# The order search of a hybrid GLA/RWKV-7 layer starts from a table of start times in the source

## Chip, core and metric

The kernel runs on one core of one Trainium2 chip. The metric is the device time of one execution in microseconds (us), the median of several runs. PE is the matmul engine (TensorE), DVE the vector engine (VectorE), ACT the scalar engine (ScalarE), POOL is GpSimd, SP is the queue engine (SyncE) that issues all DMAs here.

## Reference

One layer of a trunk with two groups of heads, on x of 4096 x 1024 in float32 (excerpt; sizes filled in):

```python
h = _rmsnorm(x, norm_w)
u = h @ w_in                          # one combined projection
# GLA group: 4 heads, key 64, value 128, chunks of 64
log_a = log_sigmoid(glr @ gate_up + gate_bias) / 16
o = _gla_chunked(q, k, v, log_a)
gla_out = rmsnorm_per_head(o) * silu(gg)
# RWKV-7 group: 8 heads of 64
mixed = cols + (prev_token(cols) - cols) * mu
r, rk, rv, wl, al = split(mixed)
# S_t = S_(t-1) (diag(w_t) - kk_t^T (a_t * kk_t)) + v_t^T k_t ;  y_t = S_t r_t
y = _rwkv7_scan(r, decay, k, v, kk, a)
rwkv_out = (groupnorm(y) + bonus) * silu(rg)
x = x + concat(gla_out, rwkv_out) @ w_out
return _rmsnorm(x, final_norm_w)
```

## The kernel before

**Tiles and stages.** The 4096 tokens go through in 8 blocks of 512. In each block the normalised x (tile `x`, two float16 halves) is multiplied by 29 tiles of 128 columns of the input weights, split into float16 high and low parts (`wr` for the RWKV group, `wg` for GLA, `wo` for the output); each projection matmul is one of three products of such halves. Weights are split once in the first 200 us, written to DRAM (`wdr`) and read back in every block through a few buffers. The RWKV group works in units of two heads: four per block, 32 in all, each of 8 chunks of 64 tokens. For a unit DVE makes `DD` (r and the normalised key with their decays) and `bk` (k and a with theirs); 16 matmuls `bank<-DD,bk` give the products within the chunks; the inverse of the delta rule's triangle is built from `Nb` and `Ta`. Then the chunks follow one upon another: `ch<-sv,DD` on PE, `us` copied out by ACT, `ch<-us,Nb`, `uv` copied out by ACT, `ch<-uv,bk`, and the new state `sv` made by DVE. That is three handovers a chunk, between PE and ACT or DVE, and each takes some time in which PE needs other matmuls to run: projections of the next block (`bank<-x,wr`, `bank<-x,wg`), or the output projection (`bank<-x,wo`). A finished block gets its residual, and its final RMSNorm, of which the last operations are eight DVE multiplies `mgg<-mgg,pkt,xacc` and `mgr<-mgr,pkt,xacc`, ahead of the store.

**What sets the order.** No instruction is emitted when it is written. Generators for the streams of work (named x, w, c, e, i, g, a, o, p, and one d for each unit; c is the chunk chain, a the projections and preparation of RWKV, p of GLA, o the output) call recording engines: every call (L473; pairs of matmuls on the two halves of the array L532) makes a `Step` with engine, a duration, and the steps that it depends on. In `build(guide)` the next stream to go on is that whose next step has the earliest start in `guide`; this decides also which buffer each tile gets. The key of a step is its stream and its number in it. Then `forward` makes a list schedule of all steps with a rank: where the array can stay in one form of matmul it prefers that by `keep`, and DVE and ACT may wait `look` us for a step of better rank; `backward` gives the latest times, which are the ranks of the next `forward`. Five such passes (`PASSES`) are made for each pair (`keep`, `look`) in `LOOKS`. The loop at the end does this for each entry of `ROUNDS`, hands the starts found to the next round as its `guide`, keeps the schedule with the earliest end by the planner's own durations, and emits the steps by their start.

Of the kernel before, what the change touches and what calls it, by code (L numbers as in the profile page):

```python
# [3 lines left out]

# [13 lines left out]
AX = mybir.AxisListType  # L18
# [3 lines left out]
P = 128  # L22
DM = 1024
KT = 8
TB = 512
C = 64
# [13 lines left out]
DL = 0.6  # L40
# [3 lines left out]
XL = 0.05  # L44
EL = 0.0
PB = {"ch": 1, "y": 1}
NBK = 6
NC = TB // C
LOOKS = ((1.0, 0.15),)
PASSES = 5  # L50
PUT_OFF = 1.0
ROUNDS = (LOOKS,) * 11
GUP = 2.0 ** 19
DECAY = math.exp(-0.5)

# [25 lines left out]
CK_GM = 896  # L81
CK_SEL = 1408
NCK = 1536


@with_exitstack
def hymba_kernel(ctx, tc, xT, wt, wg, wo, wua, gup, pk, ck, out):
    nc = tc.nc
    nc.scalar.preload_act_table_set("exp_and_others")
    NT = out.shape[1]  # L90
# [1498 lines left out]
        return steps, forward, backward  # L1589

    with tc.manual_schedule(engines={getattr(mybir.EngineType, e) for e in ("PE", "DVE", "Activation", "Pool", "SP")}):
        guide, best = {}, None
        for looks in ROUNDS:
            steps, forward, backward = build(guide)
            first_order = forward([s.t0 for s in steps])
            mine = first_order
            for keep, look in looks:
                start, end = first_order
                for _ in range(PASSES):
                    start, end = forward(backward(end), keep, look)  # L1600
                    mine = min(mine, (start, end), key=lambda x: max(x[1]))
            if best is None or max(mine[1]) < max(best[2]):
                best = (steps,) + mine
            guide = {s.key: (mine[0][s.n], mine[1][s.n]) for s in steps}
        steps, start, end = best
        for s in sorted(steps, key=lambda s: (start[s.n], s.n)):
            s.f()
# [3 lines left out]
def _layout(d):  # L1611
# [22 lines left out]
    i = np.arange(P)  # L1634
    ck = np.zeros((P, NCK), np.float32)
    ck[:64, CK_BONES] = 1
# [34 lines left out]
```

## Time and profile before

| | |
|---|---|
| time, median of three runs | 2221.82 us (2220.91 to 2226.53) |
| profiled execution | 2219.66 us, of which the profile's span is 2217.9 us |
| PE busy | 2130.2 us, mean granted clock 0.984 |
| DVE busy | 1705.3 us |
| ACT busy | 1249.9 us |
| POOL busy | 877.8 us |
| largest group on PE | `bank<-x,wr`: 6528 matmuls, 799.4 us |

Times in the profile are in us from the span's start. A row of the time line has start, length, engine, line, operation, `out<-in` by the program's names, how many instructions the row joins, and in square brackets the idle time of the engine just before it with what ended it. "PE waits for" rows give the whole idle time, how often, and the longest. The granted clock is the share of full speed at which PE ran. Lines L473 and L532 are those of the two recording helpers, so groups are told apart by tiles and not by lines.

### The profile page before, as it was taken

Reading aid. Unit: us, or ns where it says so; the run is one execution under the profiler, and the core shown is the slowest. Engines: PE = TensorE matmul, PEld = TensorE weight load, DVE = VectorE, ACT = ScalarE, POOL = GpSimd, SP = SyncE. Lnnn points to the kernel's source line nnn. Section 1 sums busy time; section 2 is a strip of 40 time slices with the busy share of each in tenths; the row PEclk is TensorE's granted clock in tenths of the full one; section 3 lists DMA queues with packets and bytes.
Section 4 is the critical chain, followed back from the end, with each engine's and each line's share of the span. In section 5 each row is a group of like instructions: output and inputs, shape, how many; then the busy total and the mean of one; then the engine's idle time right before and its main releaser. Section 6 shows DMA issues by size and latency. Waiting matters only on the chain.

```text
span 2217.9 us, 75008 instructions
## 1 busy us (share of the span) xinstructions
PE 2130.2 (96%) x30680; PEld 1365.4 (62%) x30680; DVE 1705.3 (77%) x3802; ACT 1249.9 (56%) x3229; POOL 877.8 (40%) x2212
## 2 busy tenths in 40 slices
PE   6899999999999999999999999999999999999997
PEld 2556675666755657656675566655666565755664
DVE  8988969588785777768777787858878588684976
ACT  7676675464645456455654556545465464655452
POOL 3462434525253451426425254442533525254400
PEclk8999999999999999999999999999999999999999
DMA  6786655455344643455434554345534465344443
GB/s 202 241 260 179 189 166 165 140 181 165 90 133 141 179 127 101 122 150 179 131 110 120 177 155 129 112 134 163 164 98 124 131 187 159 91 130 126 120 131 96
DMA packets 275454, 326.90 MB, mean 147 GB/s; under 512 B 131572, under 2 KB 132772, under 8 KB 275108
## 3 DMA queue, kind: packets, MB, share of 16 engines
q1 hardware_dynamic: 275108, 322.10, 49.5%
q8 instruction: 240, 3.93, 0.7%
q14 instruction: 106, 0.87, 0.1%
HBM read 276.94 MB, written 45.05 MB: 145 GB/s over the span
## 4 chain that ended last, share of the span: by engine, by line
PE 64%; DVE 19%; DMA 8%; ACT 4%; issue 3%; POOL 2%; SPq 1%; DVEq 0%; ACTq 0%; POOLq 0%
PE bank L532 51%; PE bank L473 8%; PE ch L532 3%; DMA xr<-in_xT_dram 3%; DVE DD L473 2%; DVE nta L473 1%; DVE bk L473 1%; SPq L473 1%; PE y L473 1%; DVE mgr L473 1%; DVE mgg L473 1%; PE y L532 1%; DVE x L473 1%; DMA wdr<-wo 1%; DVE Nb L473 1%
## 5 line engine op out<-in xcount | busy, mean ns | idle before, releaser
L532 PE MATMUL bank<-x,wr 128*64 128x512 f16 x6528 | 799.4, 382 | 8.2 <-ACT x L473 2.7
L473 POOL TENSOR_TENSOR tm<-Tc,f 128x60 f32<-128x60 f32 (+24 forms) x961 | 349.7, 364 | 614.3 <-DMA f<-nd 531.6
L532 PEld LDWEIGHTS <-wr 128*64 128x64 f16 x6528 | 359.8, 111 | 266.6 <-issue 30.7
L473 POOL TENSOR_TENSOR Tc<-Tc,tm 128x60 f32<-128x60 f32 (+24 forms) x961 | 361.2, 376 | 74.1
L532 PE MATMUL bank<-x,wg 128*64 128x512 f16 x3072 | 372.2, 381 | 4.6 <-DVE ki L473 2.0
L532 PE MATMUL bank<-x,wo 128*64 128x512 f16 x2976 | 354.8, 381 | 0.1
L473 POOL TENSOR_TENSOR xacc<-xacc,xr 128x512 f32<-128x512 f32 x98 | 130.3, 1330 | 365.4 <-ACT xr L473 195.8
L532 PEld LDWEIGHTS <-wg 128*64 128x64 f16 x3072 | 174.0, 110 | 123.8 <-issue 7.3
L473 DVE SCALAR_TENSOR_TENSOR sv<-ch,PC,psd 64x64 f32<-64x64 f32 x434 | 122.4, 282 | 145.9 <-PE ch L532 131.8
L532 PEld LDWEIGHTS <-wo 128*64 128x64 f16 x2976 | 161.6, 110 | 116.9 <-issue 4.3
L532 PEld LDWEIGHTS <-x 128*64 128x64 f16 x6240 | 190.1, 110 | 20.9 <-issue 9.4
L532 PE MATMUL bank<-wg,x 128*64 128x128 f16 x6144 | 196.4, 219 | 4.4 <-issue 2.7
L473 ACT ACTIVATE psd<-sv,PC 128x128 f32<-128x128 f32 x248 | 99.1, 399 | 164.6 <-DVE sv L473 142.8
L473 ACT COPY uv<-ch 64x64 f32<-64x64 f32 x496 | 101.7, 205 | 82.1 <-PE ch L532 73.2
L473 ACT COPY us<-ch 64x64 f32<-64x64 f32 x496 | 101.5, 205 | 59.0 <-PE ch L532 50.5
L473 ACT ACTIVATE sa<-bank,mu_s 128x512 f32<-128x512 f32 x104 | 71.4, 687 | 64.7 <-PE bank L532 63.2
L473 DVE COPY_PREDICATED Nb<-mc,bank 64x512 f32<-64x512 uint8 x128 | 92.9, 728 | 6.2 <-PE bank L473 4.4
L473 DVE COPY_PREDICATED DD<-mc,bank 64x512 f32<-64x512 uint8 x128 | 93.5, 731 | 2.7
L532 PEld LDWEIGHTS ch<-sv,DD 128*64 128x64 f32 x992 | 66.1, 138 | 47.0 <-DVE sv L473 15.0
L532 PEld LDWEIGHTS ch<-us,Nb 128*64 128x64 f32 x992 | 66.3, 138 | 45.8 <-ACT us L473 15.4
L532 PEld LDWEIGHTS ch<-uv,bk 128*64 128x64 f32 x992 | 66.1, 138 | 41.5 <-ACT uv L473 12.8
L473 POOL MEMSET Tc<- 32x8 f32 (+1 forms) x160 | 23.5, 147 | 165.5 <-DMA td<-Tc 160.1
(348 smaller groups left out, 3616.9 us busy)
## 6 DMA issues: line engine op xcount, KB each, us to landing
wr<-wdr SPq DMA_DIRECT2D x256, 256.0 KB
wg<-wdr SPq DMA_DIRECT2D x184, 256.0 KB
xr<-in_xT_dram SPq DMA_DIRECT2D x176, 256.0 KB
wo<-wdr SPq DMA_DIRECT2D x128, 256.0 KB
f<-nd SPq DMA_DIRECT2D x128, 128.0 KB
x<-in_wt_dram SPq DMA_DIRECT2D x29, 512.0 KB
wdr<-wo SPq DMA_DIRECT2D x25, 512.0 KB
out_dram<-mgg SPq DMA_DIRECT2D x33, 256.0 KB
```

The lines of the kernel that those rows point to most:

```text
L473: put(t0, self.name, d, lag, cols, tiles, tab, outs, ins, lambda: f(*a, **kw))
L532: nc.tensor.matmul(x, lhsT=l, rhs=y, start=start, stop=stop)
```

## The change

The starts of the first guide come from a table in the source: 25,340 differences in tenths of a us, one for each step, packed; `COUNTS` names 42 streams and how many steps each has. From it one round is made, with two pairs (`keep`, `look`) in place of one. Before, eleven rounds were made from an empty guide. The rest of the program is the same, and so is the set of steps, but buffer numbers, the order on every engine, and the waits that follow from it are new. The two helper lines L473 and L532 are L626 and L685 in the changed source.

```diff
--- before.py
+++ after.py
+import base64
 import heapq
 import math
+import struct
+import zlib
...
-LOOKS = ((1.0, 0.15),)
+LOOKS = ((0.7, 0.3), (1.0, 0.0))
 PASSES = 5
 PUT_OFF = 1.0
-ROUNDS = (LOOKS,) * 11
+ROUNDS = (LOOKS,) * 1
...
+COUNTS = ((('d', 0), 19), (('d', 1), 19), (('d', 10), 19), (('d', 11), 19), (('d', 12), 19), (('d', 13), 19), (('d', 14), 19), (('d', 15), 19), (('d', 16), 19), (('d', 17), 19), (('d', 18), 19), (('d', 19), 19), (('d', 2), 19), (('d', 20), 19), (('d', 21), 19), (('d', 22), 19), (('d', 23), 19), (('d', 24), 19), (('d', 25), 19), (('d', 26), 19), (('d', 27), 19), (('d', 28), 19), (('d', 29), 19), (('d', 3), 19), (('d', 30), 19), (('d', 31), 21), (('d', 4), 19), (('d', 5), 19), (('d', 6), 19), (('d', 7), 19), (('d', 8), 19), (('d', 9), 19), ('a', 9745), ('c', 3379), ('e', 109), ('g', 1720), ('i', 1184), ('init', 38), ('o', 2464), ('p', 4920), ('w', 603), ('x', 568))
+STARTS = (
+    "c-qZ<2b>(mv3E__+1Y&gPC1;yDN6`NL<S*11es)ljWHPv78pb@Ho-=ioQ=W4@JtRS^Wb4jwEX}R3?>;NA!A`cWFaA;yPNu|t9xd8W@p1;{64h5)6P!l>F%no`d4*z^}~({;@=o(1Q)W9p-+nbY-p!n"
...
+)
...
+def first_guide():
+
+    d = zlib.decompress(base64.b85decode(STARTS))
+    t, i, g = 0.0, 0, {}
+    for name, n in COUNTS:
+        for k in range(n):
+            t += struct.unpack_from("<h", d, 2 * i)[0] / 10
+            g[(name, k)] = (t, t + 0.3)
+            i += 1
+    return g
...
-        guide, best = {}, None
+        guide, best = first_guide(), None
         for looks in ROUNDS:
             steps, forward, backward = build(guide)
```

What moves is shown at three places; the names in the rows have the buffer's number at their end.

**Place A: the fifth block's final norm, which runs while unit 22 (counted from 0) is prepared (1523 to 1533 us in the trace of before).** DVE before, from the unit's first `bk<-ta,E` on:

```order
L473 SCALAR_TENSOR_TENSOR bk_242<-ta_198,E_197 64x8x64
L473 SCALAR_TENSOR_TENSOR sv_256<-ch_267,PC_235,psd_269 64x64 x2
L473 SCALAR_TENSOR_TENSOR mgg_0_92<-mgg_0_92,pkt_102,xacc_194 128x512
L473 SCALAR_TENSOR_TENSOR mgg_0_93<-mgg_0_93,pkt_102,xacc_194 128x512
L473 SCALAR_TENSOR_TENSOR mgg_0_94<-mgg_0_94,pkt_102,xacc_194 128x512
L473 SCALAR_TENSOR_TENSOR mgg_0_95<-mgg_0_95,pkt_102,xacc_194 128x512
L473 SCALAR_TENSOR_TENSOR mgr_0_97<-mgr_0_97,pkt_102,xacc_194 128x512
L473 SCALAR_TENSOR_TENSOR sv_256<-ch_267,PC_235,psd_269 64x64 x2
L473 SCALAR_TENSOR_TENSOR mgr_0_98<-mgr_0_98,pkt_102,xacc_194 128x512
L473 SCALAR_TENSOR_TENSOR mgr_0_99<-mgr_0_99,pkt_102,xacc_194 128x512
L473 SCALAR_TENSOR_TENSOR mgr_0_100<-mgr_0_100,pkt_102,xacc_194 128x512
L473 TENSOR_TENSOR bk_242<-kf_199,E_197 64x8x64
```

DVE in the changed kernel, from the same `bk<-ta,E` on:

```order
L626 SCALAR_TENSOR_TENSOR bk_238<-ta_198,E_197 64x8x64
L626 TENSOR_TENSOR DD_0_134<-r_200,EP_227 64x8x64
L626 TENSOR_TENSOR DD_0_134<-rn_196,EP_227 64x8x64 x2
L626 SCALAR_TENSOR_TENSOR sv_255<-ch_267,PC_228,psd_269 64x64
L626 SCALAR_TENSOR_TENSOR bk_238<-ta_198,E_197 64x8x64
L626 SCALAR_TENSOR_TENSOR gbc_231<-gbc_231,gus_116,gep_232 128x512
L626 SCALAR_TENSOR_TENSOR sv_255<-ch_267,PC_228,psd_269 64x64
L626 SCALAR_TENSOR_TENSOR gbc_231<-gmask_107,gbc_231 128x512
L626 COPY_PREDICATED Nb_0_137<-mc_103,bank_0_189 64x4x2x64
L626 COPY_PREDICATED DD_0_134<-mc_103,bank_0_189 64x8x64
L626 TENSOR_SCALAR nm_234<-gbc_231 128x4
L626 SCALAR_TENSOR_TENSOR mgg_0_92<-mgg_0_92,pkt_102,xacc_194 128x512
```

The eight multiplies `mgg` and `mgr` stood ahead of the unit's last `bk` and `DD`; now they begin behind them and behind the first `COPY_PREDICATED` rows.

PE before, at the same place, from the last projection ahead of it:

```order
L532 MATMUL bank_0_189<-x_1_3_0_90,wr_213 64x512
L532 MATMUL ch_267<-us_268,Nb_0_138 64x64 x2
L473 MATMUL bank_0_187<-DD_0_134,bk_242 128x128
L532 MATMUL ch_267<-uv_136,bk_243 64x64 x2
L532 MATMUL ch_267<-sv_256,DD_0_135 64x64 x2
L532 MATMUL ch_267<-us_268,Nb_0_138 64x64 x2
L532 MATMUL ch_267<-uv_136,bk_243 64x64 x2
L532 MATMUL ch_267<-sv_256,DD_0_135 64x64 x2
L532 MATMUL ch_267<-us_268,Nb_0_138 64x64 x2
L473 MATMUL bank_0_190<-DD_0_134,bk_242 128x128
```

PE in the changed kernel, from the handover behind the unit's `bank<-DD,bk` on:

```order
L626 MATMUL bank_0_185<-DD_0_134,bk_238 128x128
L685 MATMUL ch_267<-sv_255,DD_0_135 64x64 x2
L685 LDWEIGHTS wr_213
L685 MATMUL bank_0_186<-x_1_2_0_89,wr_213 64x512
L685 LDWEIGHTS wr_213
L685 MATMUL bank_0_186<-x_1_2_0_89,wr_213 64x512
L685 LDWEIGHTS wr_213
L685 MATMUL bank_0_186<-x_1_3_0_90,wr_213 64x512
L685 LDWEIGHTS wr_213
L685 MATMUL bank_0_186<-x_1_3_0_90,wr_213 64x512
L685 LDWEIGHTS wr_213
```

Before, seven rows of the chunk chain follow each other with one `bank<-DD,bk` among them; now projections stand between two steps of the chain.

**Place C: the end of unit 0's chunk chain, while unit 2 is prepared in the same buffers (170 to 186 us in the trace of before).** PE before, near the end of the chain:

```order
L532 MATMUL ch_267<-us_268,Nb_0_137 64x64 x2
L532 MATMUL ch_267<-uv_136,bk_242 64x64 x2
L532 LDWEIGHTS amW_210
L532 MATMUL bank_0_186<-identb_109,amW_210 64x128
L532 LDWEIGHTS amW_210
L532 MATMUL bank_0_186<-identb_109,amW_210 64x128
L532 MATMUL ch_267<-sv_255,DD_0_134 64x64 x2
L532 MATMUL ch_267<-us_268,Nb_0_137 64x64 x2
```

PE in the changed kernel, the last steps of that chain:

```order
L685 MATMUL ch_267<-us_268,Nb_0_137 64x64 x2
L685 MATMUL ch_267<-uv_136,bk_238 64x64 x2
L685 MATMUL ch_267<-sv_254,DD_0_134 64x64 x2
L685 MATMUL y_272<-DD_0_134,sv_254 64x64 x16
L685 MATMUL ch_267<-us_268,Nb_0_137 64x64 x2
L626 MATMUL y_272<-Nb_0_137,uv_136 64x64 x16
L685 MATMUL ch_267<-uv_136,bk_238 64x64 x2
L626 MATMUL bank_0_185<-crs_217,bones_105 32x128 x4
L626 MATMUL bank_0_187<-DD_0_134,bk_238 128x128
L626 MATMUL bank_0_188<-DD_0_134,bk_238 128x128
```

Before, four steps of the chain have only the two `amW` matmuls among them; now the last steps stand together, and the next unit's `bank<-DD,bk` follow the last `ch<-uv,bk` with one small group between.

**Block 7: the preparation of unit 30 (2052 to 2058 us in the trace of before).** DVE before:

```order
L473 TENSOR_TENSOR DD_0_134<-r_200,EP_234 64x8x64
L473 SCALAR_TENSOR_TENSOR sv_256<-ch_267,PC_237,psd_269 64x64 x2
L473 SCALAR_TENSOR_TENSOR rn_196<-rk_195,pkt_102,rn_196 128x512
L473 TENSOR_TENSOR DD_0_134<-r_200,EP_234 64x8x64
L473 SCALAR_TENSOR_TENSOR ta_198<-ta_198,rn_196 128x512
L473 TENSOR_TENSOR DD_0_134<-rn_196,EP_234 64x8x64 x2
L473 SCALAR_TENSOR_TENSOR bk_242<-ta_198,E_197 64x8x64 x2
L473 SCALAR_TENSOR_TENSOR sv_256<-ch_267,PC_237,psd_269 64x64 x2
```

DVE in the changed kernel:

```order
L626 SCALAR_TENSOR_TENSOR nta_209<-nta_209,nva_207 128x128
L626 SCALAR_TENSOR_TENSOR sv_255<-ch_267,PC_230,psd_269 64x64 x2
L626 SCALAR_TENSOR_TENSOR nyc_273<-nta_209,nyc_273 128x128
L626 SCALAR_TENSOR_TENSOR rn_196<-rk_195,pkt_102,rn_196 128x512
L626 TENSOR_TENSOR nta_209<-nyc_273 128x128
L626 SCALAR_TENSOR_TENSOR ta_198<-ta_198,rn_196 128x512
L626 SCALAR_TENSOR_TENSOR mgr_0_97<-bank_0_185,iv_283,xr_222 128x512
L626 SCALAR_TENSOR_TENSOR bk_238<-ta_198,E_197 64x8x64 x2
L626 SCALAR_TENSOR_TENSOR sv_255<-ch_267,PC_230,psd_269 64x64 x2
```

The four `DD` have gone further ahead, and output work (`mgr<-bank,iv,xr`) and a Newton step (`nyc`, `nta`) stand before the unit's last two `bk`.

134 lines of the change are left out of this document (added).

## The prediction

> **What bounds the kernel now.** I read the page's first part, then a table of windows of 100 us, then the waits of TensorE (PE).
>
> ```profile
> span 2217.9 us, 75008 instructions
> PE 2130.2 (96%) x30680; PEld 1365.4 (62%) x30680; DVE 1705.3 (77%) x3802; ACT 1249.9 (56%) x3229; POOL 877.8 (40%) x2212
> ...
> 0.00:100.00 100.00, 78.55 (x908) 42.17 (x910) 88.27 (x255) 73.08 (x128) 32.43 (x58) 0.91 0.68 213
> 100.00:200.00 100.00, 88.04 (x1198) 58.00 (x1194) 89.47 (x239) 68.64 (x151) 51.46 (x120) 0.91 0.73 230
> ...
> 1500.00:1600.00 100.00, 94.63 (x1372) 61.13 (x1370) 88.47 (x174) 51.58 (x127) 39.52 (x76) 0.97 0.53 162
> 2000.00:2100.00 100.00, 97.69 (x1386) 62.01 (x1380) 67.38 (x143) 47.14 (x137) 40.17 (x103) 1.00 0.44 126
> ...
> PE ch L532 <- ACT us L473: 7.8, 11, 1.7
> PE ch L532 <- DVE sv L473: 7.2, 9, 1.8
> ...
> PE ch L532 <- ACT uv L473: 3.8, 7, 0.8
> ```
>
> In a window's row stand its length, the busy time of PE, weight loads, DVE, ACT and POOL (in brackets the instructions), then the granted clock of PE, the DMA share and GB/s. PE is busy for 2130.2 of 2217.9 us, so an order of the same instructions can win no more than the 87.7 us in which PE is idle, and what PE loses at a low clock. Of the idle time 21.45 + 11.96 = 33.4 us lie in the first 200 us, where DVE is busy for 88 and 89 of 100 us; the rest lies in short waits. The largest families are the handovers of the RWKV chunk chain: a chunk goes `ch<-sv,DD`, `ch<-us,Nb`, `ch<-uv,bk` on PE, and between two of them ACT copies `us`, `uv` or DVE makes `sv`: 7.8 + 7.2 + 3.8 = 18.8 us.
>
> Every step of the program is kept: both programs have as many matmuls, 1,821 DMAs and 33 ACT table loads. So nothing is priced by instructions added or removed; the sum is over waits that lose their cause and waits that gain one.
>
> **Place A, 1526 us.** The two order pieces at A belong here.
>
> ```profile
> 1526.81 0.34 PE L532 MATMUL ch<-uv,bk 128*64 128x64 f32 x4 [0.62 <-ACT uv L473]
> 1528.03 0.34 PE L532 MATMUL ch<-sv,DD 128*64 128x64 f32 x4 [0.88 <-DVE sv L473]
> 1528.92 0.34 PE L532 MATMUL ch<-us,Nb 128*64 128x64 f32 x4 [0.56 <-ACT us L473]
> 1529.78 0.48 PE L532 MATMUL ch<-uv,bk 128*64 128x64 f32 x4 [0.52 <-ACT uv L473]
> 1532.06 0.48 PE L532 MATMUL ch<-sv,DD 128*64 128x64 f32 x4 [1.79 <-DVE sv L473]
> 1533.13 0.48 PE L532 MATMUL ch<-us,Nb 128*64 128x64 f32 x4 [0.59 <-ACT us L473]
> ...
> 1523.95 2.74 DVE L473 SCALAR_TENSOR_TENSOR mgg<-mgg,pkt,xacc 128x512 f32<-128x512 f32 x4
> 1526.61 0.74 DVE L473 SCALAR_TENSOR_TENSOR mgr<-mgr,pkt,xacc 128x512 f32<-128x512 f32 x1
> 1528.00 2.08 DVE L473 SCALAR_TENSOR_TENSOR mgr<-mgr,pkt,xacc 128x512 f32<-128x512 f32 x3
> 1530.11 0.69 DVE L473 TENSOR_TENSOR bk<-kf,E 64x512 f32<-64x512 f32 x1
> 1531.92 1.16 DVE L473 SCALAR_TENSOR_TENSOR bk<-ta,E 64x512 f32<-64x512 f32 x1
> ...
> 1526.00:1533.00 7.00, 2.16 (x22) 1.18 (x20) 6.86 (x13) 3.54 (x13) 1.71 (x1) 0.76 1.02 351
> 1533.00:1537.00 4.00, 3.87 (x38) 3.64 (x40) 3.90 (x6) 1.74 (x5) 1.91 (x2) 0.57 0.31 104
> ```
>
> PE runs two chunks bare, with no other matmul between the handovers, until the unit's `bank<-DD,bk` can go on. Those need `bk` and `DD`, which DVE makes only behind eight final-norm multiplies (2.74 + 0.74 + 2.08 = 5.56 us). The waits add to 0.62 + 0.88 + 0.56 + 0.52 + 1.79 + 0.59 = 4.96 us. The new order has all `DD` and `bk` ahead of the multiplies, and projection matmuls between the handovers: **-4.96 us**. The multiplies feed only the store of a finished block, so what is late next is that store, on which no matmul waits before the end.
>
> The clock falls with it: 0.76 and 0.57 were granted in the two windows. A clock of c costs (1 - c) of the busy time: 0.24 x 2.16 + 0.43 x 3.87 = 2.18 us, which I count as going with the waits, since PE then has work throughout: **-2.18**. From the other side the term is 0, if the clock falls there for another reason.
>
> In the Trainium skill, "TensorE: Matmul & The Clock Gate", section "Part 1: The HAM clock gate (the "warmup" mystery)", says that PE returns to half rate after at least one idle window, of about 3.4 us. Taken literally, the rule gives these waits no share in the low clock, for the longest is 1.79 us, and the sum would lose both clock terms; the trace does not agree with so literal a reading, for the clock fell in a window in which PE worked 2.16 of 7.00 us and was never idle for 3.4 us on end.
>
> **Place B, 725 us**, is of the same kind.
>
> ```profile
> 725.32 0.34 PE L532 MATMUL ch<-us,Nb 128*64 128x64 f32 x4 [0.31 <-ACT us L473]
> 726.34 0.34 PE L532 MATMUL ch<-uv,bk 128*64 128x64 f32 x4 [0.69 <-ACT uv L473]
> 727.72 0.79 PE L473 MATMUL bank<-DD,bk 64*128 64x128 f32 x2 [1.04 <-DVE bk L473]
> ...
> 729.45 0.48 PE L532 MATMUL ch<-us,Nb 128*64 128x64 f32 x4 [0.54 <-ACT us L473]
> ...
> 727.00:734.00 7.00, 5.75 (x42) 4.76 (x44) 6.74 (x11) 1.86 (x6) 1.28 (x1) 0.53 0.47 143
> ```
>
> The new order puts about 1 us of projections or more into each of these handovers and `bank<-DD,bk` 3 us later against DVE. Waits 0.31 + 0.69 + 1.04 + 0.54: **-2.58**. Clock 0.47 x 5.75: **-2.70**, from the other side 0.
>
> **Place C, 170 us**, in the stretch where weights are still being split.
>
> ```profile
> 170.37 0.34 PE L532 MATMUL ch<-us,Nb 128*64 128x64 f32 x4 [0.66 <-ACT us L473]
> 171.53 0.34 PE L532 MATMUL ch<-uv,bk 128*64 128x64 f32 x4 [0.83 <-ACT uv L473]
> 173.00 0.25 PE L532 MATMUL bank<-identb,amW 128*64 128x128 bf16 x2 [1.13 <-ACT wo L473]
> ...
> 174.02 0.34 PE L532 MATMUL ch<-us,Nb 128*64 128x64 f32 x4 [0.55 <-ACT us L473]
> 175.38 1.07 PE L532 MATMUL bank<-x,wg 128*64 128x512 f16 x4 [1.03 <-DVE ki L473]
> ...
> 182.53 3.19 PE L532 MATMUL bank<-x,wg 128*64 128x512 f16 x28
> ...
> 182.75 1.39 DVE L473 TENSOR_TENSOR bk<-kf,E 64x512 f32<-64x512 f32 x2
> 184.15 1.41 DVE L473 SCALAR_TENSOR_TENSOR bk<-ta,E 64x512 f32<-64x512 f32 x2
> ```
>
> Five waits of 0.66 + 0.83 + 1.13 + 0.55 + 1.03 = 4.20 us get projections ahead of them. But the 3.19 us of `bank<-x,wg` that now stand behind the unit's last `ch<-uv,bk` are gone from there: in the new order four small `bank<-crs,bones` and then `bank<-DD,bk` follow it, while DVE cannot start `bk` before that `ch<-uv,bk` has read the old one, and needs 1.39 + 1.41 = 2.80. That is a new wait of about 2.6, and two handovers next to it become bare. A bare handover I price at 0.6, the median of the twelve handover waits quoted from A, B and C (0.31 to 1.79). New: 2.6 + 1.2 = 3.8; net **-0.4**, with -4.2 and +3 as ends.
>
> **Single places.** Two waits lose their cause, as more work stands between the maker and the reader than the reader waited:
>
> ```profile
> 2062.58 1.05 PE L532 MATMUL bank<-x,wr 128*64 128x512 f16 x8 [1.44 <-DVE v L473]
> ...
> 2138.72 0.34 PE L532 MATMUL ch<-sv,DD 128*64 128x64 f32 x4 [0.94 <-DVE sv L473]
> ```
>
> **-2.38.** Of 705 handovers, 18 have under 0.3 us of matmuls between them before, and 9 after; four of these nine stand alone at places that had cover: 4 x 0.6 = **+2.4** (0 to 1.79 each).
>
> **Block 7, 2058 and 2091 us.**
>
> ```profile
> 2055.86 1.39 DVE L473 SCALAR_TENSOR_TENSOR bk<-ta,E 64x512 f32<-64x512 f32 x2
> ...
> 2058.60 2.06 PE L473 MATMUL bank<-DD,bk 64*128 64x128 f32 x32
> ...
> 2091.65 1.61 PE L473 MATMUL bank<-DD,bk 64*128 64x128 f32 x24 [0.23 <-DVE bk L473]
> ```
>
> By the durations of the trace `bank<-DD,bk` at 2058 comes 5.3 us of PE's work earlier (some 25 projections), and DVE has 1.1 us more to do ahead of it, a `mgr<-bank,iv,xr` among it; before, the first `bk` was made by 2056.55 (half of the DVE row's 1.39 us) and read at 2058.60, a slack of 2.05. So it is up to 5.3 + 1.1 - 2.05 = 4.4 us short. At 2091 the shortfall is up to 4.9 (1.3 earlier, 3.7 more on DVE). DVE is idle for 32.6 of the 100 us there and can make up most of it. Bounds 0 and 9.3; I take a third, **+3**, since DVE waits mostly for transfers that are themselves issued by their place in the order.
>
> The head is taken at **0**: its 33.4 us stay, as DVE is the bound there with the same work; the orders of the weight splits differ by some us both ways, so -5 to +5. All other places move by less than 5 us of PE's work and are taken at 0; SP's queue of reloads is the rival below.
>
> **Sum:** -4.96 - 2.18 - 2.58 - 2.70 - 0.4 - 2.38 + 2.4 + 3 = -9.8 us. The profiled execution took 2219.66 us (the span is 2217.9), so 2209.9; the median of the runs is 2221.82, 2.16 above the profiled one, so **2212 us**. About 0.3% (6.7 us) is what a measurement of this kernel can tell from no change: the bounds are 2215.2 and 2228.5.
>
> **Rivals.**
> (1) The waits only move. A unit's chain is a fixed row of 24 handovers, and cover given to one is taken from another; the exchange at C is an instance. If A and B are paid back in full elsewhere, only the clock terms and D stay: -4.9 - 2.4 + 5.4 for the new waits = -1.9, some 2220. Against it: the bare handovers halve.
> (2) A larger gain. If every handover gets its cover, the three families of 18.8 us go whole, with B's wait for `bk` (1.04), the wait for `v` (1.44) and the 4.88 of the clock, and nothing new comes: 26.2, or 2196. For it: the same halving. Against it: nine remain, and PE's program is full, so that cover is taken from elsewhere.
> (3) Slower: DVE comes late at `bank<-DD,bk`. PE reaches the first of them earlier against DVE at four units (6.4 and 5.0 us at 2058 and 2091, 4.0 at 996, 3.0 at 1794). If DVE makes up nothing, the waits are 9.3 + 4.0 + 3.0 = 16.3, of which 3 are counted, and a low clock behind each costs as at A and B (4 x 2.44 = 9.8): -9.8 + 13.3 + 9.8 = +13.3, or 2235. It decides where DVE's idle time in the 10 us ahead is under the shortfall. Against it: its 32.6 us of idle time in that window.
> (4) The clock term is not tied to the waits: 2212 + 4.9 = 2217. The low clock stands right at the waits of A and B, and the window 2000:2100, without such a row of waits, was granted 1.00, which speaks against it. The rule that the Trainium skill gives on that page would have it so.
> (5) A reload of weights lands too late: the least PE work between the last reader of a weight buffer and the next use of it falls from 4.2 to 3.5 us, and 11 places instead of 3 have under 4.4. About 11 x 0.5 = 5.5 at most, or 2217.
> (6) The change does not do what it says. The new order is in the program, so this is left only as an order that differs and is worth the same: it goes with (1).
>
> **How the numbers follow.** Forecast 0.43 (2206 to 2217, nearly all below 2215.2), larger gain 0.18, waits that move with (5) 0.22, clock not tied 0.05, slower 0.12. Faster by over 0.3%: 0.40 + 0.18 = 0.58; within: 0.03 + 0.22 + 0.05 = 0.30; slower: 0.12. The range goes from 2194, which leaves out some 0.05 of the larger gain, to 2226, which leaves out the 0.12 of slower.
>
> **What would show it.** A: no wait over 0.3 us on `ch` between the last multiplies of the fifth block and the unit's `bank<-DD,bk`, and a granted clock of 1.00 there. B: the same, with `bank<-DD,bk` not waiting for `bk`. C: one wait of 2 to 3 us on `bank<-DD,bk` near 180 us for DVE `bk`. Block 7: a wait on `bank<-DD,bk` of 0 to 4 us at two places. Busy PE time falls by about the 4.9 us of the clock, the rest of the gain is idle time. The forecast is wrong if the head's 33.4 us change by more than 5, if low-clock windows stand at new places, or if waits for `wr` and `wg` come up.

## The result and the profile after

The changed kernel took 2208.62 us (median of 5 runs, 2204.48 to 2210.6) beside 2220.91 us for the kernel before (5 runs, 2218.74 to 2226.53): a ratio of 0.9939, 95% interval [0.9922, 0.9956]. The forecast was 2212 us, a ratio of 0.9956. The profiled execution took 2207.91 us, 11.75 us less than the profiled one of before; the sum of the prediction was -9.8.

The first lines of the page after, and PE's waits by what ended them (total us, times, longest):

```profile
span 2206.1 us, 75003 instructions
PE 2119.0 (96%) x30680; PEld 1352.7 (61%) x30680; DVE 1711.7 (78%) x3802; ACT 1253.8 (57%) x3229; POOL 875.1 (40%) x2212
...
PE bank L626 <- DVE bk L626: 8.9, 7, 4.0
PE bank L685 <- ACT wo L626: 5.6, 6, 2.8
PE bank L685 <- DMA wg<-wdr: 4.9, 5, 1.9
...
PE ch L685 <- ACT uv L626: 4.5, 6, 1.3
PE ch L685 <- ACT us L626: 4.3, 7, 1.8
PE bank L626 <- POOL xacc L626: 3.3, 3, 1.2
...
PE bank L626 <- DVE DD L626: 1.9, 2, 1.6
...
PE ch L685 <- DVE sv L626: 1.7, 2, 1.4
```

The same families before, as far as they were not shown:

```profile
PE bank L473 <- DVE DD L473: 5.9, 4, 4.0
...
PE bank L473 <- DVE bk L473: 3.3, 4, 1.0
...
PE bank L532 <- DMA wg<-wdr: 2.4, 4, 0.8
...
PE bank L532 <- ACT wo L473: 1.6, 2, 1.1
```

The surprise is in the first two lines. PE's idle time is 2206.1 - 2119.0 = 87.1 us, and was 87.7: **the new order has as much idle time as the old one.** The handovers of the chunk chain did fall in this execution, from 18.8 to 4.5 + 4.3 + 1.7 = 10.5 us. But waits for the split of `wo` rose by 4.0, for `wg` by 2.5, for `bk` or `DD` from 3.3 + 5.9 = 9.2 to 8.9 + 1.9 = 10.8, and 3.3 for `xacc` are new. (`bk` and `DD` are taken together: a wait of 4.0 us at 112 us is put down to `DD` before, and one of 4.0 at 118 us to `bk` after.)

A second profile of the changed kernel (c_after, below) shows how little of this is fixed. There the handovers add to 9.2 + 5.0 + 4.6 = 18.8 us, as before the change, and PE is idle for 2206.4 - 2116.4 = 90.0 us:

```profile
PE 2116.4 (96%) x30680; PEld 1348.5 (61%) x30680; DVE 1711.2 (78%) x3802; ACT 1251.7 (57%) x3229; POOL 872.0 (40%) x2212
...
PE ch L685 <- ACT us L626: 9.2, 7, 3.2
...
PE ch L685 <- ACT uv L626: 5.0, 8, 1.5
...
PE ch L685 <- DVE sv L626: 4.6, 6, 2.1
```

What fell in both profiles is the busy time, by 11.2 and 13.8 us with the same matmuls: PE ran at a higher clock (0.993 and 0.990 against 0.984). Windows around the stretches in which less than full clock was granted (columns as in the prediction: length, busy PE, weight loads, DVE, ACT, POOL, clock), before:

```profile
41.00:49.00 8.00, 5.43 (x36) 2.12 (x38) 7.77 (x31) 7.91 (x12) 0.00 (x0) 0.57 0.28 73
113.00:124.00 11.00, 9.70 (x86) 8.57 (x88) 10.31 (x26) 4.54 (x7) 9.35 (x22) 0.53 0.63 195
174.00:182.00 8.00, 6.95 (x88) 4.72 (x90) 6.99 (x19) 7.79 (x22) 0.16 (x1) 0.57 0.76 247
386.00:390.00 4.00, 4.00 (x26) 1.76 (x23) 3.87 (x11) 2.91 (x5) 0.49 (x3) 0.57 0.32 49
727.00:735.00 8.00, 6.75 (x50) 5.31 (x52) 7.74 (x12) 2.45 (x7) 1.28 (x1) 0.57 0.49 150
806.00:810.00 4.00, 4.00 (x26) 1.76 (x22) 2.14 (x7) 0.00 (x0) 3.06 (x13) 0.58 0.53 175
1529.00:1537.00 8.00, 5.09 (x50) 4.34 (x52) 7.84 (x12) 3.53 (x10) 3.62 (x3) 0.57 0.68 237
2140.00:2148.00 8.00, 7.67 (x112) 5.18 (x112) 6.65 (x16) 7.71 (x19) 0.00 (x0) 0.57 0.38 84
```

and after, with place A for comparison in the last row:

```profile
113.00:124.00 11.00, 6.14 (x50) 4.91 (x52) 9.69 (x22) 5.30 (x10) 9.43 (x21) 0.69 0.88 272
180.00:191.00 11.00, 8.81 (x84) 7.04 (x86) 10.70 (x20) 8.78 (x24) 0.91 (x6) 0.53 0.55 168
1310.00:1314.00 4.00, 4.00 (x30) 2.37 (x28) 3.91 (x7) 1.48 (x5) 1.44 (x3) 0.57 0.32 89
1903.00:1908.00 5.00, 5.00 (x126) 4.72 (x128) 4.88 (x8) 1.81 (x4) 0.00 (x0) 0.66 0.54 167
...
1526.00:1533.00 7.00, 6.99 (x76) 3.73 (x74) 6.88 (x14) 6.13 (x18) 0.00 (x0) 1.00 0.63 199
```

(1 - clock) times PE's busy time gives 2.3 + 4.6 + 3.0 + 1.7 + 2.9 + 1.7 + 2.2 + 3.3 = 21.7 us before and 1.9 + 4.1 + 1.7 + 1.7 = 9.4 after: 12 us, about the whole difference between these two executions. Two stretches are left out: that between 13 and 27 us, which the trace of after does not record (see the last section), and the end, where PE has 0.3 us of work or none.

The higher clock is not one lucky execution: the mean clock of before was 0.986, 0.987 and 0.986 in three batches of 29, 18 and 23 runs, that of the changed kernel 0.991 and 0.990 in two of 5 and 7. But over many executions the clock gives less than in this pair. Where both kernels have their clocks in one batch on one chip (that of c_after), the means are 0.990 and 0.987, and 0.003 of 2207 us is some 6.5 us at most (PE is not busy in all of it), of the 11 us that the ratio 0.9951 stands for. The profiled execution of before, at 0.984, lies low among executions of 0.983 to 0.990. So over many executions the clock stands for about half of the gain; what the rest is, the record does not settle.

### The profile page after: what moved, and what is told of

Its sections match the earlier page's. It is cut to its first block, busy times and chain, and to the rows that moved or that the text cites. A ratio compares the mean times of both kernels' runs of the same rounds, so it can differ in the third digit from the quotient of the medians.

```text
span 2206.1 us, 75003 instructions
## 1 busy us (share of the span) xinstructions
PE 2119.0 (96%) x30680; PEld 1352.7 (61%) x30680; DVE 1711.7 (78%) x3802; ACT 1253.8 (57%) x3229; POOL 875.1 (40%) x2212
## 4 chain that ended last, share of the span: by engine, by line
PE 66%; DVE 16%; DMA 9%; issue 2%; ACT 2%; SPq 2%; POOL 2%; DVEq 0%; POOLq 0%; ACTq 0%
PE bank L685 52%; PE bank L626 8%; PE ch L685 4%; DMA xr<-in_xT_dram 2%; SPq L626 2%; DVE DD L626 2%; DVE nta L626 1%; DVE bk L626 1%; PE y L626 1%; DMA rn<-bcda 1%; DMA x<-in_wt_dram 1%; PE y L685 1%; DVE mgg L626 1%; DVE x L626 1%; DVE Nb L626 1%
## 5 line engine op out<-in xcount | busy, mean ns | idle before, releaser
L685 PE MATMUL bank<-x,wr 128*64 128x512 f16 x6528 | 796.2, 380 | 7.2 <-ACT x L626 1.4
L626 POOL TENSOR_TENSOR tm<-Tc,f 128x60 f32<-128x60 f32 (+24 forms) x961 | 347.7, 362 | 589.0 <-DMA f<-nd 507.2
L685 PEld LDWEIGHTS <-wr 128*64 128x64 f16 x6528 | 356.1, 110 | 260.1 <-issue 22.1
L626 POOL TENSOR_TENSOR Tc<-Tc,tm 128x60 f32<-128x60 f32 (+24 forms) x961 | 358.2, 373 | 74.1
L685 PE MATMUL bank<-x,wg 128*64 128x512 f16 x3072 | 367.1, 381 | 3.0 <-DMA wg<-wdr 1.9
L685 PE MATMUL bank<-x,wo 128*64 128x512 f16 x2976 | 357.2, 380 | 0.0
L626 POOL TENSOR_TENSOR xacc<-xacc,xr 128x512 f32<-128x512 f32 x98 | 130.8, 1334 | 359.5 <-ACT xr L626 227.9
L685 PEld LDWEIGHTS <-wg 128*64 128x64 f16 x3072 | 169.4, 110 | 126.3 <-issue 5.0
L626 DVE SCALAR_TENSOR_TENSOR sv<-ch,PC,psd 64x64 f32<-64x64 f32 x434 | 122.5, 282 | 160.1 <-PE ch L685 140.6
L685 PEld LDWEIGHTS <-wo 128*64 128x64 f16 x2976 | 159.2, 110 | 112.4 <-issue 2.9
L685 PEld LDWEIGHTS <-x 128*64 128x64 f16 x6240 | 190.1, 111 | 20.8 <-issue 9.0
L685 PE MATMUL bank<-wg,x 128*64 128x128 f16 x6144 | 195.4, 220 | 4.6 <-DMA wg<-wdr 3.0
L626 ACT ACTIVATE psd<-sv,PC 128x128 f32<-128x128 f32 x248 | 98.9, 399 | 139.4 <-DVE sv L626 108.3
L626 ACT COPY uv<-ch 64x64 f32<-64x64 f32 x496 | 102.3, 206 | 76.5 <-PE ch L685 69.5
L626 ACT COPY us<-ch 64x64 f32<-64x64 f32 x496 | 102.2, 206 | 67.8 <-PE ch L685 57.7
L626 ACT ACTIVATE sa<-bank,mu_s 128x512 f32<-128x512 f32 x104 | 71.6, 689 | 73.5 <-PE bank L685 71.1
L626 DVE COPY_PREDICATED Nb<-mc,bank 64x512 f32<-64x512 uint8 x128 | 92.8, 728 | 13.1 <-PE bank L626 11.3
L626 POOL MEMSET Tc<- 32x8 f32 (+1 forms) x160 | 24.2, 151 | 186.1 <-DMA td<-Tc 180.7
L626 DVE COPY_PREDICATED DD<-mc,bank 64x512 f32<-64x512 uint8 x128 | 93.3, 731 | 2.3
L685 PEld LDWEIGHTS ch<-uv,bk 128*64 128x64 f32 x992 | 66.1, 137 | 44.1 <-ACT uv L626 10.9
L685 PEld LDWEIGHTS ch<-us,Nb 128*64 128x64 f32 x992 | 65.4, 137 | 43.0 <-ACT us L626 11.0
L685 PEld LDWEIGHTS ch<-sv,DD 128*64 128x64 f32 x992 | 65.0, 136 | 40.0 <-DVE sv L626 7.3
```

What stands on the lines that cost most here:

```text
L626: put(t0, self.name, d, lag, cols, tiles, tab, outs, ins, lambda: f(*a, **kw))
L685: nc.tensor.matmul(x, lhsT=l, rhs=y, start=start, stop=stop)
```

## The experiments

Every ratio is to the kernel before, run beside it on the same chip.

| run | what it is | us | ratio, 95% interval |
|---|---|---|---|
| e1_norm_ahead | changed, eight multiplies back ahead | 2213.09 | 0.9968 [0.9951, 0.9984] |
| e2_norm_behind | before, eight multiplies behind | 2232.79 | 1.0053 [1.0033, 1.0073] |
| h1_head_before | head of before, rest changed | 2221.59 | 0.9987 [0.9970, 1.0003] |
| h2_head_after | head changed, rest of before | 2223.01 | 1.0009 [0.9993, 1.0025] |
| g1_place_A | before, place A changed | 2220.89 | 1.0009 [0.9995, 1.0024] |
| c_after | the changed kernel again | 2206.85 | 0.9951 [0.9931, 0.9970] |
| p_looks_alone | new LOOKS, no table, 11 rounds | 2201.86 | 0.9922 [0.9905, 0.9938] |
| p_table_alone | table, old LOOKS, 1 round | 2205.68 | 0.9941 [0.9920, 0.9963] |
| f_fill | before, idle PE filled at A and B | 2215.65 | 0.9980 [0.9963, 0.9997] |
| i_looks_05 | other LOOKS, no table, 7 rounds | 2196.05 | 0.9890 [0.9864, 0.9915] |
| i_looks_07 | other LOOKS, by table | 2211.26 | 0.9956 [0.9937, 0.9974] |
| i_fill | i_looks_05, idle PE filled in the head | 2196.61 | 0.9881 [0.9851, 0.9912] |

In the first two and in the runs with filling, steps are emitted by a copy of the schedule's starts, `place`, in which a few are changed; a step still waits for all that it depends on.

### Is the DVE order at A the cause of the waits there?

```diff
+        for i in range(8):
+            place[("o", 1484 + 2 * i)] = place[("a", 6813)] - 0.01 + 0.001 * i
```

> The changed kernel, with only the fifth block's eight final-norm multiplies put back on DVE, ahead of the unit's two DD<-rn. Theory (place A: these 5.56 us of DVE make PE wait for DD and bk, and the low clock follows the wait): one wait of about 5.5 us on bank<-DD,bk near 1523 us, a low-clock stretch behind it (some 2 us), and 2208.6 + 5.5 to 8, so 2214 to 2217. Rival (waits only move, so an added wait is taken from later ones): the wait is there, but the time stays within 2 us of 2208.6.

PE in the changed order with the multiplies put back, and the window there:

```profile
1522.04 0.79 PE L626 MATMUL bank<-DD,bk 64*128 64x128 f32 x2 [4.40 <-DVE DD L626]
...
1523.75 3.78 PE L626 MATMUL bank<-DD,bk 64*128 64x128 f32 x30 [0.35 <-DVE bk L626]
...
1520.00:1528.00 8.00, 5.61 (x42) 4.51 (x44) 7.59 (x14) 0.51 (x2) 0.00 (x0) 0.57 0.01 2
```

The wait came (4.40 + 0.35) and the low clock came with it (0.43 x 5.61 = 2.4 us): the last thirty `bank<-DD,bk`, 2.05 us at full clock, take 3.78. So at this place the order on DVE is the cause of the wait. What it costs in the end is less clear. The median is 2213.09 us, just under the 2214 to 2217 expected, and by the ratios 4 to 6 us above the changed kernel (0.9968 beside 0.9951 and 0.9939, on other chips), but the interval overlaps that of 0.9951. And the profiled execution took 2209.17 us, only 1.3 more than that of the changed kernel, with PE idle for 85.1 us instead of 87.1: there the added wait was made up elsewhere. The rival, that later waits swallow it, is not ruled out.

The opposite, the kernel before with the multiplies put behind:

```diff
+        for i in range(8):
+            place[("o", 1484 + 2 * i)] = place[("a", 6827)] + 0.01 + 0.001 * i
```

> The kernel before, with only the same eight multiplies moved on DVE behind the COPY_PREDICATED rows of that unit; PE's order is that of before. Theory as predicted (the multiplies are the cause at A): the 4.96 us of waits fall to 1 to 2 us, the low clock at 1530 us goes, 2220.9 - 5 to 6, so about 2215. Rival (PE's bare order is the cause: each handover without matmuls between costs about 0.6 us whatever DVE does): only the waits of 0.88 and 1.79 fall to 0.6, -1.5 us, the six waits add to about 3.5, the low clock stays, 2219.

Both expected times were missed. PE and ACT at A:

```profile
1526.94 0.34 PE L532 MATMUL ch<-sv,DD 128*64 128x64 f32 x4 [0.75 <-DVE sv L473]
...
1529.78 0.48 PE L532 MATMUL ch<-sv,DD 128*64 128x64 f32 x4 [0.75 <-DVE sv L473]
...
1551.73 0.48 PE L532 MATMUL ch<-us,Nb 128*64 128x64 f32 x4 [9.36 <-ACT us L473]
...
1540.11 0.63 ACT L473 ACTIVATE xacc<-xr 128x512 f32<-128x512 f32 x1 [8.30 <-DVE mgr L473]
...
1544.18 1.31 ACT L473 ACTIVATE xr<-xr 128x512 f32<-128x512 f32 x2 [3.44 <-DMA xr<-in_xT_dram]
...
1549.06 0.63 ACT L473 ACTIVATE xr<-xr 128x512 f32<-128x512 f32 x1 [3.28 <-DMA xr<-in_xT_dram]
```

Of the six waits only the two on DVE shrank (0.88 and 1.79 to 0.75 each); the four of 0.52 to 0.62 us stayed, so 4.96 became 3.79, and the low clock stayed at 1529 us, both as the rival had it. A bare handover costs its 0.5 to 0.75 us here whatever DVE does. And a new wait of 9.36 us came, which neither had. The multiplies read `xacc`, and the next block's first ACT operation overwrites it, so `xacc<-xr` waits 8.30 us for them. The next load of `xr` is issued right behind it, at 1540.76 us (1530.77 in the kernel before). ACT then waits 3.44, 3.28 and 0.90 us for such loads, and the copies `us` of the chain stand behind these operations in ACT's order. In the changed kernel that `xacc<-xr` stands behind the chain's copies. So the order on DVE alone does not make A, as PE and ACT have another order there too; whether one of those alone would is not shown.

### Does a stretch carry its gain with it?

Three kernels take order and buffers from one kernel in some stretches and from the other elsewhere. They make no search: `STARTS` and `ENDS` are tables that give out the buffers, and `PLACES` is one for the order, with the values of both kernels joined at the seams.

```diff
+        first, last_, place = table(STARTS, 500000), table(ENDS, 500000), table(PLACES, 500000)
+        steps = build({k: (first[k], last_[k]) for k in first})[0]
```

> Order and buffers of before in the first 340 us (up to the 34,729 last rows of PE, which are those of the changed kernel), and of the changed kernel from there. By PE's work done the changed kernel is 3.2 us later than before at this point. Theory (the gains lie at places, independent of the head): the rest runs as in the changed kernel, 2208.6 - 3.2, about 2205.5, with waits at A of about 0.7 and the same few low-clock stretches (1310 and 1904 us). Rival (what was gained is the place of the clock's windows, which any shift changes): low-clock stretches stand elsewhere and in another number, 2208 to 2216.

> The opposite: order of the changed kernel in the first 340 us, of before from there. Theory: 2220.9 + 3.2, about 2224, waits of about 2.6 and 5 us at B and A and a low clock at 386, 727, 806, 1530 and 2140 us as before. Rival: as many waits, but low-clock stretches at other places, 2214 to 2224.

> The kernel before, with order and buffers of the changed kernel in one stretch around place A alone (1440 to 1630 us, all engines), and of before elsewhere. Theory (A is a place by itself: order of DVE, ACT and PE together takes 4.3 us of waits and one low-clock stretch away): 6 to 7 us less than before, 2221 to 2223 become 2215 to 2216; the low clock at 1530 us is gone. Rival (waits only move: what is won there is lost in the stretch behind, or at the seams): within 2 us of before.

All three ended level with before: h1 missed both its ranges, h2 came where its theory and its rival both put it, and g1 within 2 us, as its rival had it. But the seams cost as much as was to be tested. In h1 a chain runs bare at the seam, with a wait of 2.17 us for `sv` at 354 us. Step for step it is 3.3 us behind the kernel before ahead of the seam, and behind the seam 9.4 us later than the changed kernel (from 409 to 470 us), where 3.2 earlier was expected. Behind the seam its low clock stands at 491, 747, 1027 and 1826 us and not at 1310 and 1904; that of h2 stands at 731, 1530 and 2144 us as in the kernel before, but not at 386 and 806. In g1 the waits at A are gone (0.17 and 0.51 are left) and the clock is 1.00 throughout, but `uv` comes 3.03 us late at the second seam, and the clock falls there.

```profile
1516.00:1540.00 24.00, 22.66 (x246) 13.82 (x242) 22.71 (x42) 13.47 (x39) 1.27 (x1) 1.00 0.58 188
...
1631.50 0.34 PE L1351 MATMUL ch<-uv,bk 128*64 128x64 f32 x4 [3.03 <-ACT uv L1292]
```

As a verdict on the whole time these three are inconclusive; what they show is local, that the change at A does at A what it did in the changed kernel, and that these schedules were not cut and joined at no cost.

### Which part of the change finds the order?

```diff
-LOOKS = ((1.0, 0.15),)
+LOOKS = ((0.7, 0.3), (1.0, 0.0))
```

> The change's two kinds of list schedule alone: the kernel before with its eleven rounds from an empty guide and the new LOOKS, no table. The planner ends at 2142.6 us by its own durations, against 2161.2 for before and 2145.6 for the changed kernel; it has 7 handovers with under 0.3 us of matmuls between them (22 before, 10 in the changed kernel, counted alike). Theory (bare handovers, and the low clock that follows them, set the time): as fast as the changed kernel or better, 2204 to 2210. Rival (the table is what matters; the planner's end says little at this scale): 2212 to 2222.

> The table alone: the changed kernel with one round and the old LOOKS. The planner ends at 2145.6 as with the new ones, with 7 bare handovers; 1115 rows of PE stand otherwise. Theory (the table carries the order, the two list schedules matter little in a single round): within 3 us of the changed kernel. Rival (small differences of order change the waits and the clock by as much as the change): 4 us or more apart.

> The changed kernel again, beside the others on one chip: 2206 to 2211, ratio 0.992 to 0.996. The theory of the clock says that its mean granted clock over the runs is about 0.991 against 0.986 of before, which is 0.005 x 2220 = 11 us of busy time; its rival (waits, not clock) says that the clocks are within 0.002.

In p_looks_alone this is the only line changed in the kernel before; p_table_alone is the changed kernel with the line turned back. The table alone is as fast as the whole change (0.9941 beside 0.9951 in the same batch), so the new pairs do nothing that can be told in the last round. The pairs alone, with the old eleven rounds and no table, are as fast or a little faster (0.9922 [0.9905, 0.9938] beside 0.9951 [0.9931, 0.9970]). So either part finds such an order without the other; how the values of the table were found is not on record. The changed kernel itself took 2206.85 us, as expected. Its mean clock, 0.990 beside 0.987, lies between its two theories, 0.005 apart and within 0.002.

### Is it the clock?

The kernel before in its own order, with useless products put into the idle time at A and B:

```diff
+            for _ in range(fill.get(s.key, 0)):
+                for h in (slice(0, 64), slice(64, 128)):
+                    nc.tensor.matmul(spare[s.key][h], lhsT=identb[:, h], rhs=identb, start=True, stop=True)
             s.f()
```

> The kernel before in its own order, with idle time of PE at A and B filled: ahead of the ten waiting matmuls stand 106 pairs of 64x128 bf16 products of the identity into a bank that is overwritten next (about 0.055 us a pair). No wait can get shorter by this. Theory (the low clock follows PE's lack of work in the waits): no low-clock stretch at 727 and 1530 us, DD,bk there in 2.05 us instead of 3.4 to 3.8, so 4 to 5 us less at the two places, 2219 to 2215. Rival (the clock falls there for another reason, or waits for what PE does not make): the stretches stay, time 0 to 2 us more than before.

PE at A in the kernel before, and then with the filling, with the window there:

```profile
1533.54 3.41 PE L473 MATMUL bank<-DD,bk 64*128 64x128 f32 x30
```

```profile
1529.37 1.62 PE L1624 MATMUL bank<-identb 128*64 128x128 bf16 x52
...
1532.71 2.05 PE L473 MATMUL bank<-DD,bk 64*128 64x128 f32 x30
...
1529.00:1537.00 8.00, 7.20 (x138) 5.63 (x136) 7.81 (x13) 3.25 (x9) 3.55 (x3) 1.00 0.62 215
```

The chain is not quicker between its steps (at A 1.2, 0.9, 0.9 and 2.3 us from one `ch` to the next, with the filling and without), and the kernel does 212 matmuls more. But the clock stays at 1.00, the products `bank<-DD,bk` take 2.05 us instead of 3.41 at A and 3.78 at B, and the kernel gets faster: 0.9980 [0.9963, 0.9997], some 4.4 us where 4 to 5 were expected. The interval, 0.7 to 8 us, is wide, so the price of the low clock is better read from these rows. Its cause at A and B is PE's lack of work: nothing else was changed, and with PE's order of before the clock falls there in every other profile (at A in before, h2 and e2, at B in these and g1).

### A better order

> No table; seven rounds from an empty guide with the pairs (0.5, 0.3) and (1.0, 0.0). The planner's end is 2136.5, against 2161.2 (before), 2145.6 (changed) and 2142.6 (LOOKS alone); 7 bare handovers. Theory (the planner's end, with bare handovers, foretells the time to a few us): 15.6 us less in the plan came to 12 on the chip and 18.6 to 17, so 24.7 come to 20 to 23, 2197 to 2200. Rival (below 2150 the plan says nothing more; clock and DMA landings decide): 2200 to 2210.

> Another order of the same search, pairs (0.7, 0.3) and (0.7, 0.0), round 36, put in by its table. The planner's end is 2139.1, but 10 bare handovers, with two more around 2140 us. Theory as for the other: 2199 to 2203. Rival: 2203 to 2212.

> The order of i_looks_05 with the same filling at its two low-clock places of the head: 91 pairs of products of the identity, ahead of the first two bank<-DD,bk that wait near 114 us and of five matmuls of the chunk chain and of amW between 170 and 175 us. Theory (low clock follows lack of work; half of 6.1 and of 5.7 us of busy time was lost there): no low-clock stretch at 115 and 173 us, 5 to 6 us less than i_looks_05, 2190 to 2192, ratio about 0.987. Rival (DVE sets the end of the head, so that PE's faster pace there is only waited away): the stretches go, but the next waits for DVE grow by as much, 2195 to 2198.

The first is two lines in the kernel before:

```diff
-LOOKS = ((1.0, 0.15),)
+LOOKS = ((0.5, 0.3), (1.0, 0.0))
...
-ROUNDS = (LOOKS,) * 11
+ROUNDS = (LOOKS,) * 7
```

It beats both kernels: 2196.05 us, 0.9890 [0.9864, 0.9915]. Its planned end foretold it to 1 us (2197 to 2200). That of i_looks_07 did not: 2139.1 us in the plan, 2.6 more than i_looks_05 and 6.5 less than the changed kernel, and on the chip 2211, no better than the changed kernel. It has 10 bare handovers by a common count, as the changed kernel has, and i_looks_05 has 7; two points do not make a rule of that. Filling the head of i_looks_05 (i_fill) gave nothing that can be told from it. The low clock at 115 us went, but others came at 177 and 191 us, and the run has a fault of its own: its last filling waited 1.26 us itself for DVE (`pw`). The time is in the range of the rival there, but whether DVE sets the end of the head stays open.

## Why the prediction was right

The time was inside the range and near the forecast, but the two halves of the sum were each off and made up for it, which is luck. Its waits came to -4.9 and measured -0.6; its clock terms came to -4.9 and the clock gave about -12, in the two profiled executions that are compared here. Of the prediction's own signs of being wrong two came: low clock at new places (1310 and 1903 us), and waits for `wg` (2.4 to 4.9 us). And it had put most of the gain into idle time, not into busy time.

- **A, waits -4.96: -4.3.** The chain has its cover, one bare handover of 0.66 is left:

```profile
1533.66 0.34 PE L685 MATMUL ch<-uv,bk 128*64 128x64 f32 x4 [0.66 <-ACT uv L626]
```

The cause was told too narrowly: e2 shows that the multiplies alone were not it. It also shows that more than the store hangs on them: the next block's `xacc<-xr` and loads of `xr` come behind them, and in e2 a matmul of the chain waited 9.36 us for that.
- **A, clock -2.18: right. B, clock -2.70: right in this execution only.** No low clock stands at A or B in the two profiles of the changed kernel, and none at A in h1 and g1, which have its order there; f_fill and e1 give about 2.2 and 2.4 us for such a stretch, from both sides. But e1 and h1 have the order of the changed kernel at B, and there the clock falls behind a wait for `bk`, for 3.4 us each, about 1.7 us lost. In e1:

```profile
734.88 3.16 PE L626 MATMUL bank<-DD,bk 64*128 64x128 f32 x30 [1.19 <-DVE bk L626]
```

So the new order takes the low clock away at B in two of four profiles.
- **The rival that the clock is not tied to the waits** fell with f_fill, and with it the literal reading of the rule in the Trainium skill, "TensorE: Matmul & The Clock Gate", section "Part 1: The HAM clock gate (the "warmup" mystery)", that half rate follows an idle window of about 3.4 us: in f_fill and in the kernel before no wait there is longer than 1.79 us, and the clock fell in the one and not in the other.
- **The clock elsewhere, taken at 0: about -7.** This is the step that was too small. The windows at 41 us (2.3) and 2140 us (3.3) went as well, and I had looked at the clock only at A and B. The one at 2140 us stands behind the very wait of 0.94 us that I counted at 2138. Both belong to the order: every profiled kernel that keeps these parts of before has them (41 to 44 us in e2, h1, g1 and f_fill, 2140 to 2154 us in e2, h2, g1 and f_fill), and no profile with the changed kernel's order there does (its own two, e1, and h2 at 41 or h1 at 2140 us). Those at 386 and 806, and after at 1310 and 1903, come and go between executions that have the same order there.
- **B, waits -2.58: +1.3.** All was paid back and more within 13 us, by handovers that became bare and a `bk` that came late (0.19 + 0.82 + 1.11 + 1.78 = 3.9 for the 2.58 removed):

```profile
733.24 0.34 PE L685 MATMUL ch<-uv,bk 128*64 128x64 f32 x4 [0.82 <-ACT uv L626]
...
735.10 2.05 PE L626 MATMUL bank<-DD,bk 64*128 64x128 f32 x30 [1.11 <-DVE bk L626]
...
745.17 0.34 PE L685 MATMUL ch<-us,Nb 128*64 128x64 f32 x4 [1.78 <-ACT us L626]
```

- **C, net -0.4: +0.3.** An even trade, with the wait on `bk` where it was put, though shorter and with more around it (0.53 + 1.38 + 0.20 + 0.42 + 0.44 + 1.55 = 4.5 for the 4.2 removed):

```profile
176.19 0.34 PE L685 MATMUL ch<-uv,bk 128*64 128x64 f32 x4 [0.53 <-ACT uv L626]
177.90 0.34 PE L685 MATMUL ch<-sv,DD 128*64 128x64 f32 x4 [1.38 <-DVE sv L626]
...
179.38 0.34 PE L685 MATMUL ch<-us,Nb 128*64 128x64 f32 x4 [0.20 <-ACT us L626]
180.13 2.20 PE L626 MATMUL y<-Nb,uv 64*64 64x64 f32 x32 [0.42 <-ACT uv L626]
...
183.18 0.66 PE L626 MATMUL bank<-crs,bones 128*32 128x128 f32 x8 [0.44 <-ACT crs L626]
185.39 2.94 PE L626 MATMUL bank<-DD,bk 64*128 64x128 f32 x18 [1.55 <-DVE bk L626]
```

- **Block 7, +3: +0.8.** DVE made up nearly all. The first place, at 2043 us now, has no wait; the second has one:

```profile
2079.34 0.48 PE L626 MATMUL bank<-DD,bk 64*128 64x128 f32 x2 [0.78 <-DVE bk L626]
```

- **Single places, -2.38: gone as put.** The head and all other places, taken at 0, and the single handovers, taken at +2.4, came to about +3.7 together (what is left of -0.6). The head is as much by itself: its idle time went from 33.4 to 37.4 us, C's +0.3 among it, with `wo` in the waits above. This is the first rival, that the waits only move, and for the idle time it held: 87.7 to 87.1 us, and 90.0 in the second profile. What it had wrong is that the time would then stay.
- **Other rivals.** The larger gain did not come from this order, though an order of the same search reached its 2196. DVE at `bank<-DD,bk` (`bk` and `DD` 10.8 us in all, 9.2 before) cost far less than the slower case needed. Reloads rose by about 3 us (`wg` 2.4 to 4.9), short of their 5.5.

## What to carry to other kernels

Where PE is busy for 96% of the time and its idle time is in many short waits, ask of each wait not only how long it is but whether the clock falls behind it: a chain of small matmuls run bare cost 2.6 to 5 us in waits here and 2 to 3 more at half clock. Read the granted clock in windows over the whole span before forecasting, not only at the places that the change is seen to mend, and read it in more than one execution. An order is one thing on all engines: the same eight DVE operations cost 5 us in waits ahead and 9 us behind, because ACT's order belonged to one of the two, and a good stretch cut out of one schedule lost its gain at the seams.

## What the hardware showed

Useless work made a kernel faster: 106 pairs of products in idle time kept the clock at 1.00 at A and B and gave 0.2% (0.03 to 0.37%).

The low clock comes in steps, which I had not seen when I forecast. In the clock records of all fourteen traces it is 0.50, and each stretch but the one at the end lasts 3.4 us or a multiple of it (6.8, 10.2 or 13.7). Within one execution all stretches start on one grid of 3.41 us: in the kernel before they start at 41.4, 113.1, 174.5 and 386.1 us, which is 21, 18 and 62 steps apart. In another execution the grid lies elsewhere. In that trace PE had work for 14 to 54% of the step just ahead of each of the eight stretches above, and for 63% or more of every step outside the stretches from 30 to 2150 us. In other traces the border is less sharp (after the change a step with 45% at 900 us was not followed by a fall, and one with 80% ahead of 1310 us was). A wait that lies in one step in one execution can be split over two in the next; that would account for stretches that come and go with the same order, but no run tests it.

The granted clock in the trace is not complete in the head: after the change the window from 20 to 27 us reads 1.00, while ten `bank<-x,wr` took 1.95 us there, 0.38 us a pair from start to start; from 30 us on a pair takes 0.22. In c_after the record has a stretch at half clock from 13.2 to 26.9 us.

Executions of one order differ by up to 15 us (2214.82 to 2229.8 for the kernel before in one batch), about the size of this change, so that a single pair of runs would have told little.

```profile
25.18 1.95 PE L685 MATMUL bank<-x,wr 128*64 128x512 f16 x10
...
20.00:27.00 7.00, 5.61 (x28) 2.04 (x25) 6.33 (x9) 4.95 (x8) 4.96 (x6) 1.00 0.51 129
```
